# Second attention: mean squares as products of high and low parts for seven heads, each head's rows normalised in two halves

## The chip, the core and the metric

The kernel runs on one core of a Trainium2 chip. The metric is the time of one execution on the device in microseconds (us). A core has a matrix engine (PE), a vector engine (DVE), a scalar engine (ACT), a general engine (POOL) and SP, which here only issues transfers (DMA). Each engine works through its own list of instructions in order; an instruction whose input or whose buffer is not ready holds up everything behind it on that engine.

## The reference, cut to what matters

Two layers: one with latent attention, one with differential attention, each followed by a gated feed-forward layer; 1024 rows, width 1024, everything in 32 bits. The part touched is in the differential attention:

```python
a = p[:, 0] - lam * p[:, 1]                     # two softmax maps per head
o = jnp.einsum('bhqk,bkhe->bqhe', a, v)         # 8 heads, 128 values each
o = _rmsnorm(o, g_sub) * (1.0 - lambda_init)    # per row and head
# _rmsnorm: o * rsqrt(mean(o*o, axis=-1) + 1e-6) * g
return o.reshape(b, s, 1024) @ w_o
```

## The kernel before

**Products.** The matrix engine is used with two formats. A product of full 32-bit operands ("f32") and one of operands rounded to a shorter format ("fp32r") go by the same instruction; the kernel gets its accuracy from the second kind by splitting an operand into a high part (a cast, made by ACT) and a low part (the difference, made by DVE or POOL) and adding three products.

**Second attention.** It takes up 1127 to 1552 us of the span. For each of 8 heads there are 8 blocks of 128 query rows. `score_b(h, i)` makes the scores of block i for the two maps: matmuls into banks `s` (L220), a DVE instruction that adds the bias, finds the extreme and writes a score tile `l` (L223), an exponential on ACT (L228), a reciprocal of the sums (DVE L1425), a scaling of map 1 (POOL L1426) and the difference of the maps (DVE L1427), which leaves the weights of the block in the tile of map 0. `turn_b` transposes them on PE (L148) into `pt`; ACT and DVE split these into `pth` (L251) and `ptl` (L252). `mix_b` makes the value product of two blocks, a "row pair" (L263, `o_b`), and DVE copies it to `bo` (L1436). `attention()` emits the scores two blocks ahead of the transposes, and hands other work to numbered slots, one behind each block: projections of the next head (`bp`, L143 to L145) and the values of the next pair of heads (`bv`, same lines). Slot 8h+i lies behind block i of head h. What runs when is set by a scheduler that orders each engine's instructions by its own planned times; the order is fixed when the kernel is built.

**Norm.** `norm_b(h)` at slot 8h+9 squares the 128x1024 outputs of a head (ACT L1451, two instructions of 512 columns) into a tile `sq`; `norm_b2(h)` at slot 8h+10 sums over the partitions with a matmul against `ones`, a 128x128 matrix of 1/128, in f32 (L1457, `ms`, in banks `s`), takes logarithm and exponential on ACT (L1460, L1462) and multiplies on POOL (L1463), which is the last reader of `sq`. SP then stores the rows of heads 0 to 5. The last head is normalised in smaller parts at the end.

**Buffers.** The score tiles of both maps and the tiles `sq` come from one pool of five buffers, `lp`, tag `l`, 128x1024 each:

```python
lp = st.enter_context(tc.tile_pool(name="b1l", bufs=5, reuse_waits="tile"))
l = lp.tile([P, 1024], F32, tag="l", name=f"l_{name}")      # softmax_block
t = lp.tile([P, S], F32, tag="l", name=f"sq{h}_{g0}")       # norm_b
```

A score tile of map 1 is free after L1427, one of map 0 after its last transpose, a tile `sq` after the POOL multiplication. An instruction that writes a tile waits for the last reader of the buffer's tile before it.

Of the kernel before, what the change touches and what calls it, by code (L numbers as in the profile page):

```python
# [9 lines left out]
F32 = mybir.dt.float32  # L10
F32R = mybir.dt.float32r
AF = mybir.ActivationFunctionType
ALU = mybir.AluOpType
# [3 lines left out]
P = 128  # L17
S = 1024
# [3 lines left out]
H = 8  # L22
# [20 lines left out]
def trunk(  # L43
# [33 lines left out]
    V, A, G, T = nc.vector, nc.scalar, nc.gpsimd, nc.tensor  # L77

    cp = ctx.enter_context(tc.tile_pool(name="cp", bufs=1))
    sp = ctx.enter_context(tc.tile_pool(name="sp", bufs=8))  # L80

    ident = cp.tile([P, P], F32, tag="ident", name="ident")
    ones = cp.tile([P, P], F32, tag="ones", name="ones")
    cst = cp.tile([P, 48], F32, tag="cst", name="cst")
    edge = ctx.enter_context(tc.tile_pool(name="edge", bufs=1, side="right"))
    edge.tile([P, 504], F32, tag="edge", name="edge")
# [20 lines left out]
    def f32(t):  # L107
        return t.bitcast(F32)
# [1059 lines left out]


    gs, nlam = cst[:, 16:17], cst[:, 24:25]  # L1170
    V.memset(ones, 1.0 / P)

    def constants():
        nc.gpsimd.dma_start(gs, g_sub)
        V.tensor_scalar(gs, gs, 1.0 - LAMBDA_INIT, None, ALU.mult)
        t = wp.tile([P, 5, 64], F32, tag="wr", name="lv", bufs=2)
        for i, src in enumerate((lam_q1, lam_k1, lam_q2, lam_k2)):
            nc.gpsimd.dma_start(t[:, i], src.partition_broadcast(P))
        dots = t[:, 4, :2]
        for i in range(2):  # L1180
            V.tensor_tensor(t[:, 2 * i], t[:, 2 * i], t[:, 2 * i + 1], ALU.mult)
            V.tensor_reduce(dots[:, i:i + 1], t[:, 2 * i], mybir.AxisListType.X, ALU.add)
        A.activation(dots, dots, AF.Exp)
        V.tensor_tensor(nlam, dots[:, 1:2], dots[:, 0:1], ALU.subtract)
        V.tensor_scalar(nlam, nlam, -LAMBDA_INIT, None, ALU.add)


    with ast as st:
        pool = st.enter_context(tc.tile_pool(name="a1", bufs=2, reuse_waits="tile"))
        vp = st.enter_context(tc.tile_pool(name="a1v", bufs=12, side="right", reuse_waits="tile"))  # L1190
        lp = st.enter_context(tc.tile_pool(name="a1l", bufs=4, side="right", reuse_waits="tile"))
# [3 lines left out]
        vt, qr, qn, kn, wts, lt, pts = {}, {}, {}, {}, {}, {}, {}  # L1195
# [90 lines left out]
        def at(slot, fn, *args):  # L1286
            fill.setdefault(slot, []).append(lambda: fn(*args))
# [57 lines left out]
    with ExitStack() as st:  # L1345
# [2 lines left out]
        ptp = st.enter_context(tc.tile_pool(name="b1p", bufs=4, reuse_waits="tile"))  # L1348
        bb = pool.tile([P, S], F32, tag="bb", name="bb", bufs=1)
        nc.sync.dma_start(bb, c_bias_b)  # L1350
        vt, lt, pts, sqs, q_slot = {}, {}, {}, {}, {}
        qt = [big_tile(f"bq{j}") for j in range(2)]
        kt = [big_tile(f"bk{j}") for j in range(2)]
        ob = big_tile("bo", F32)
# [90 lines left out]
        def norm_b(h, g0=0, g1=4):  # L1445

            t = lp.tile([P, S], F32, tag="l", name=f"sq{h}_{g0}")
            sqs[h, g0] = [(t[:, (g - g0) * 256:min(g + 2, g1) * 256 - g0 * 256],
                           o_rows(h, g, min(2, g1 - g))) for g in range(g0, g1, 2)]
            for sq, o in sqs[h, g0]:  # L1450
                A.activation(sq, o, AF.Square)  # L1451

        def norm_b2(h, g0=0, g1=4):
            parts = []
            for i, (sq, o) in enumerate(sqs.pop((h, g0))):
                m = ps_s(f"ms{h}_{g0}_{i}")[:, :sq.shape[1]]
                T.matmul(m, ones, sq, start=True, stop=True)  # L1457
                parts.append((sq, o, m))
            for r, _, m in parts:
                A.activation(r, m, AF.Ln, bias=eps_rms, scale=1.0)  # L1460
            for r, o, _ in parts:
                A.activation(r, r, AF.Exp, scale=-0.5)  # L1462
                G.tensor_tensor(o, o, r, ALU.mult)  # L1463
            if h < H - 2:
                for g in range(g0, g1):
                    nc.sync.dma_start(o_dr[1][g][h], o_rows(h, g))
# [34 lines left out]
                for slot, tb in ((1, 0), (3, 1), (6, 2), (7, 3), (8, 4), (9, 5), (10, 6), (13, 7)):  # L1501
                    at(b + slot, values_b, h // 2, tb)
        for h in range(H - 1):
            at(8 * h + 9, norm_b, h)
            at(8 * h + 10, norm_b2, h)
        at(8 * H - 6, norm_b, H - 1, 3, 4)
        at(8 * H - 5, norm_b2, H - 1, 3, 4)
        at(8 * H - 4, norm_b, H - 1, 2, 3)
# [113 lines left out]
```

## Time and profile before

| what | value |
|---|---|
| time, median of 3 runs | 2267.78 us (2267.59 to 2267.83) |
| the profiled execution: its time | 2268.24 us |
| the profiled execution: its span in the trace | 2266.5 us, so 1.74 us lie around it |
| mean granted clock of TensorE | 0.998 of full speed |
| second attention in the span | 1127 to 1552 us |
| projection of its output, then the last feed-forward layer | from about 1505 us to the end |

The rows further down are from the profiled execution. An instruction's time there is from its start to its end, and matmuls overlap: the start of one to the start of the next is shorter than the duration printed for it. A full f32 matmul appears as two records.

### The profile page before, as it was taken

Reading aid. Unit: us, or ns where it says so; the run is one execution under the profiler, and the core shown is the slowest. Engines: PE = TensorE matmul, PEld = TensorE weight load, DVE = VectorE, ACT = ScalarE, POOL = GpSimd, SP = SyncE. Lnnn points to the kernel's source line nnn. Section 1 sums busy time; section 2 is a strip of 40 time slices with the busy share of each in tenths; the row PEclk is TensorE's granted clock in tenths of the full one; section 3 lists DMA queues with packets and bytes.
Section 4 is the critical chain, followed back from the end, with each engine's and each line's share of the span. In section 5 each row is a group of like instructions: output and inputs, shape, how many; then the busy total and the mean of one; then the engine's idle time right before and its main releaser. Section 6 shows DMA issues by size and latency. Waiting matters only on the chain.

```text
span 2266.5 us, 31066 instructions
## 1 busy us (share of the span) xinstructions
PE 2240.2 (99%) x11410; PEld 1912.8 (84%) x11410; DVE 1542.9 (68%) x2894; ACT 1014.3 (45%) x2097; POOL 773.9 (34%) x626
## 2 busy tenths in 40 slices
PE   8999999999999999999999999999999999999998
PEld 8999998888888888888888898878788888888886
DVE  5676765696766667767576667576686656668778
ACT  4365564352333334444465656564442333334444
POOL 3232341114444440455432424221114444430551
PEclk9999999999999999999999999999999999999999
DMA  5010125434435338454320212063334223238443
GB/s 203 11 37 31 42 70 186 143 127 151 174 130 204 114 129 327 183 192 158 98 52 22 68 34 64 21 223 126 125 138 163 90 103 107 100 112 324 165 180 150
DMA packets 105545, 287.76 MB, mean 127 GB/s; under 512 B 7968, under 2 KB 30112, under 8 KB 94896
## 3 DMA queue, kind: packets, MB, share of 16 engines
q1 hardware_dynamic: 101552, 277.44, 34.5%
q0 software_dynamic: 3840, 8.33, 1.4%
q8 instruction: 90, 1.47, 0.3%
q14 instruction: 63, 0.52, 0.1%
HBM read 204.47 MB, written 77.07 MB: 124 GB/s over the span
## 4 chain that ended last, share of the span: by engine, by line
PE 94%; DVE 2%; DMA 1%; issue 1%; ACT 1%; POOL 0%; SPq 0%; DVEq 0%; POOLq 0%; ACTq 0%
PE gb L548 15%; PE gc L548 10%; PE ga L548 10%; PE dw L872 7%; PE dx L872 5%; PE s_a L220 4%; PE zp_a L418 3%; PE s_b L220 3%; PE dv L872 3%; PE dy L872 3%; PE bp L145 3%; PE bp L143 3%; PE bp L144 3%; PE o_a L263 2%; PE o_b L263 2%; PE hq L1121 1%
## 5 line engine op out<-in xcount | busy, mean ns | idle before, releaser
L504 ACT CAST op_g<-gr 128x512 fp32r<-128x512 f32 x240 | 146.8, 621 | 376.9 <-PE gb L548 190.6
L505 POOL TENSOR_TENSOR op_g<-gr,op_g 128x512 fp32r<-128x512 f32 x104 | 145.5, 1404 | 255.3 <-ACT op_g L504 149.5
L505 DVE TENSOR_TENSOR op_h<-rh,op_h 128x512 fp32r<-128x512 f32 x152 | 140.7, 951 | 51.5 <-ACT op_h L504 51.5
L548 PE MATMUL ga<-xh_m,op_g 128*128 128x512 f32 x512 | 168.2, 389 | 0.0
L872 PE MATMUL dw<-op_w_t,op_h 128*128 128x512 f32 x660 | 151.1, 390 | 0.0
L504 ACT CAST op_h<-rh 128x512 fp32r<-128x512 f32 x152 | 91.9, 619 | 127.2 <-PE dx L872 35.0
L872 PEld LDWEIGHTS dw<-op_w_t,op_h 128*128 128x128 f32 x660 | 123.7, 188 | 25.6
L228 ACT ACTIVATE l_b<-l_b,mx_b 128x256 f32<-128x256 f32 (+7 forms) x128 | 99.4, 777 | 73.1 <-DVE mx_b L223 71.4
L505 POOL TENSOR_TENSOR op_w_b<-rw_b,op_w_b 128x512 fp32r<-128x512 f32 x44 | 64.4, 1488 | 172.9 <-ACT op_w_b L504 165.7
L505 DVE TENSOR_TENSOR op_g<-gr,op_g 128x512 fp32r<-128x512 f32 x136 | 111.7, 825 | 16.8 <-ACT op_g L504 16.4
L872 PE MATMUL dx<-op_w_b,op_h 128*128 128x512 f32 x528 | 121.5, 390 | 1.0 <-DVE op_w_b L505 1.0
L1426 POOL TENSOR_SCALAR l_b<-l_b,rb,cst 128x128 f32<-128x128 f32 (+3 forms) x64 | 52.5, 821 | 199.3 <-DVE rb L1425 187.9
L872 PEld LDWEIGHTS dx<-op_w_b,op_h 128*128 128x128 f32 x528 | 98.8, 188 | 23.0 <-DVE op_w_b L505 2.6
L548 PE MATMUL gb<-t3h_f,op_g 128*128 128x512 f32 x352 | 115.4, 389 | 1.4 <-DVE tmp L637 1.4
L548 PE MATMUL gb<-t2h_f,op_g 128*128 128x512 f32 x352 | 115.4, 390 | 0.4 <-DVE op_g L505 0.4
L548 PE MATMUL gc<-t1h_f,op_g 128*128 128x512 f32 x352 | 115.6, 389 | 0.0
L548 PE MATMUL gb<-t4h_f,op_g 128*128 128x512 f32 x352 | 115.5, 389 | 0.0
L548 PE MATMUL gc<-b22h_f,op_g 128*128 128x512 f32 x352 | 115.3, 389 | 0.0
L548 PEld LDWEIGHTS ga<-xh_m,op_g 128*128 128x128 f32 x512 | 96.1, 188 | 19.9
L505 POOL TENSOR_TENSOR op_g<-s,op_g 128x512 fp32r<-128x512 f32 x40 | 55.3, 1381 | 167.9 <-ACT op_g L504 159.8
L143 PE MATMUL bp<-xT_f,h_wb 128*128 128x512 f32 x256 | 101.7, 397 | 0.0
L144 PE MATMUL bp<-xT_f,h_wb 128*128 128x512 f32 x256 | 101.6, 397 | 0.0
(388 smaller groups left out, 6688.6 us busy)
## 6 DMA issues: line engine op xcount, KB each, us to landing
gr<-in_w_gu SPq DMA_DIRECT2D x44, 1024.0 KB, 6.9
rh<-h_dr SPq DMA_DIRECT2D x28, 1024.0 KB, 4.9
h_dr<-sh SPq DMA_DIRECT2D x22, 1024.0 KB, 4.9
h_dr<-hp SPq DMA_DIRECT2D x22, 768.0 KB, 4.2
tt<-in_w_dn SPq DMA_DIRECT2D x22, 512.0 KB, 7.6
rh<-h_dr SPq DMA_DIRECT2D x12, 768.0 KB, 4.4
wo_dr<-op_pwo SPq DMA_DIRECT2D x16, 512.0 KB, 3.5
z<-xs_dr SPq DMA_DIRECT2D x16, 512.0 KB, 11.5
```

Of the source, the lines that this page charges most:

```text
L143: T.matmul(ps_out, lh, rh, start=(i == 0), stop=False)
L144: T.matmul(ps_out, lh, rl, start=False, stop=False)
L145: T.matmul(ps_out, ll, rh, start=False, stop=(i == n - 1))
L220: T.matmul(s[:, :w], lh, rh[:, ks], start=(j == 0), stop=(j == len(q_pass) - 1))
L228: ends["exp"] = A.activation(l[:, :n], l[:, :n], AF.Exp, bias=mx, scale=-1.0, accum_out=sm).ins
L263: T.matmul(po[:, c], a, b[:, j % 2, c], start=st, stop=sp_, skip_group_check=True)
L418: T.matmul(m, a[:, h, :], self.wo[h][w][:, c], start=(start and h == heads[0] and a is oh and w == 0), stop=(stop and h == heads[-1] and a ...
L504: turns["cast"] = A.copy(hi, src).ins
L505: return eng.tensor_tensor(lo, src, f32(hi), ALU.subtract).ins
L548: T.matmul(o, w[:, a, k * P:(k + 1) * P], x[b][:, k, :], start=(first and k == 0 and (a, b) == (0, 0)), stop=(k == 3 and a == 1), skip_gro ...
L872: T.matmul(o, h[:, a, c], w[:, b_], start=(first and (a, b_) == (0, 0)), stop=(last and a == 1), skip_group_check=True,).ins for a, b_ in ...
L1426: G.tensor_scalar(l1[:, :n], l1[:, :n], r[:, 1:2], nlam, ALU.mult, ALU.mult)
```

## The change

Three things. `ones` becomes an fp32r tile, written by a DVE instruction from `ident` in `constants()` instead of a memset. For heads 0 to 6, each 512 columns of squares are split into a cast (ACT, L1455 of the new kernel) and a difference (DVE, L1456) in a second tile `sqhl` from the same pool `lp`; two fp32r matmuls (L1464) take the place of the f32 one. And each of these heads is normalised in two halves: row pairs 0 and 1 at slots 8h+5 and 8h+6, row pairs 2 and 3 at 8h+9 and 8h+10. A half holds 512 columns, but each of its two tiles takes a whole buffer of `lp`. The last head keeps its parts and the f32 product.

```diff
-    ones = cp.tile([P, P], F32, tag="ones", name="ones")
+    ones = cp.tile([P, P], F32R, tag="ones", name="ones")
...
-    V.memset(ones, 1.0 / P)
...
     def constants():
+        V.tensor_scalar(ones, ident, 0.0, 1.0 / P, ALU.mult, ALU.add)
...
             for sq, o in sqs[h, g0]:
                 A.activation(sq, o, AF.Square)
+                if h < H - 1:
+                    hl = lp.tile([P, S], F32R, tag="l", name=f"sqhl{h}_{g0}")
+                    hi, lo = sq_hl[h, g0] = hl[:, :512], hl[:, 512:]
+                    A.copy(hi, sq)
+                    V.tensor_tensor(lo, sq, f32(hi), ALU.subtract)
...
                 m = ps_s(f"ms{h}_{g0}_{i}")[:, :sq.shape[1]]
-                T.matmul(m, ones, sq, start=True, stop=True)
+                if h < H - 1:
+                    for k, part in enumerate(sq_hl.pop((h, g0))):
+                        T.matmul(m, ones, part, start=(k == 0), stop=(k == 1))
+                else:
+                    T.matmul(m, f32(ones), sq, start=True, stop=True)
...
         for h in range(H - 1):
-            at(8 * h + 9, norm_b, h)
-            at(8 * h + 10, norm_b2, h)
+            for i in range(2):
+                at(8 * h + (5, 9)[i], norm_b, h, 2 * i, 2 * i + 2)
+                at(8 * h + (6, 10)[i], norm_b2, h, 2 * i, 2 * i + 2)
```

The scheduler orders the whole stage anew. Two places are shown here: PE and DVE where head 1 ends, and ACT where head 6 ends. In the names, `s_b_2_0_0` is the scores of block 2, map 0, bank 0; `l_b_7_0` the tile of block 7, map 0; `pt_b_7_0` the first four transposes of block 7; the number at the end is a running number.

PE of the kernel before, where head 1 ends and head 2 begins, from the last value projections to the transposes of block 7 of head 1:

```order
L143 MATMUL bv_3_11751<-h_wbv_1_11218,xT_f_10050 128x256
L144 MATMUL bv_3_11751<-l_wbv_1_11219,xT_f_10050 128x256
L145 MATMUL bv_3_11751<-h_wbv_1_11218,xT_f_10051 128x256
L220 MATMUL s_b_2_0_0_11809<-bk_10191,bq_10189 128x384
L220 MATMUL s_b_2_0_0_11809<-bk_10191,ql_10194 128x384
L148 MATMUL pt_b_7_0_11733<-ident,l_b_7_0_11516 128x128 x4
```

PE of the changed kernel at the same place, from the scores of block 0 of head 2 to the same transposes:

```order
L220 MATMUL s_b_0_1_0_11636<-bk_10191,bq_10189 128x128
L220 MATMUL s_b_0_1_0_11636<-bk_10191,ql_10194 128x128
L1464 MATMUL ms_0_0_11728<-sqhl_0_11603,ones 128x512 x2
L220 MATMUL s_b_1_0_0_11739<-bk_10191,bq_10189 128x256
L220 MATMUL s_b_1_0_0_11739<-bk_10191,ql_10194 128x256
L220 MATMUL s_b_1_1_0_11746<-bk_10191,bq_10189 128x256
L220 MATMUL s_b_1_1_0_11746<-bk_10191,ql_10194 128x256
L220 MATMUL s_b_2_0_0_11831<-bk_10191,bq_10189 128x384
L220 MATMUL s_b_2_0_0_11831<-bk_10191,ql_10194 128x384
L148 MATMUL pt_b_7_0_11755<-ident,l_b_7_0_11525 128x128 x4
```

Before, 24 value projections (`bv_3`) stand between the scores of blocks 1 and 2 of head 2; in the changed kernel they stand earlier, and the matmuls of the first half's norm stand there instead.

DVE of the changed kernel at the same place, from the norm's difference to the difference of the maps of block 7:

```order
L1456 TENSOR_TENSOR sqhl_0_11603<-sq_0_11601,sqhl_0_11603 128x512
L252 TENSOR_TENSOR ptl_b_6_0_11651<-pt_b_6_0_11645,pth_b_6_0_11650 128x2x128
L1425 RECIPROCAL rb_7_11524<-smb_7_11523 128x2
L1436 COPY bo<-o_b_2_11606 128x256
L223 ISA l_b_0_0_11628,mx_b_0_0_0_11632<-s_b_0_0_0_11629,bb 128x128
L223 ISA mx_b_0_0_0_11632 128x1
L252 TENSOR_TENSOR ptl_b_6_1_11655<-pt_b_6_0_11645,pth_b_6_1_11654 128x2x128
L252 TENSOR_TENSOR ptl_b_6_2_11663<-pt_b_6_1_11658,pth_b_6_2_11662 128x2x128
L223 ISA l_b_0_1_11635,mx_b_0_1_0_11639<-s_b_0_1_0_11636,bb 128x128
L223 ISA mx_b_0_1_0_11639 128x1
L1427 SCALAR_TENSOR_TENSOR l_b_7_0_11525<-l_b_7_0_11525,rb_7_11524,l_b_7_1_11537 128x1024
```

The score tile `l_b_0_1` written by the last L223 lies in the buffer that held `sqhl_0_11603`; the difference of the maps of block 7 stands right behind it. Before, the buffer of that tile was one of block 6 of head 1, and L1456 was not there.

ACT of the kernel before, at the end of head 6, between the two exponentials of its block 7:

```order
L228 ACTIVATE l_b_7_0_14798,smb_7_14796<-l_b_7_0_14798,mx_b_7_0_1_14807 128x1024
L251 CAST pth_b_6_0_14922<-pt_b_6_0_14917 128x2x128
L1378 CAST bvh_7_14864<-bv_7_14839 128x256
L406 ACTIVATE oh_a_7_14957<-of_a_7_14955,cst 128x768
L228 ACTIVATE l_b_7_1_14810,smb_7_14796<-l_b_7_1_14810,mx_b_7_1_1_14819 128x1024
```

ACT of the changed kernel at the same place:

```order
L228 ACTIVATE l_b_7_0_14852,smb_7_14850<-l_b_7_0_14852,mx_b_7_0_1_14861 128x1024
L251 CAST pth_b_6_0_14981<-pt_b_6_0_14976 128x2x128
L1451 ACTIVATE sq_0_14922<-bo 128x512
L1378 CAST bvh_7_14918<-bv_7_14893 128x256
L406 ACTIVATE oh_a_7_15022<-of_a_7_15020,cst 128x768
L1455 CAST sqhl_0_14924<-sq_0_14922 128x512
L228 ACTIVATE l_b_7_1_14864,smb_7_14850<-l_b_7_1_14864,mx_b_7_1_1_14873 128x1024
```

The square and the cast of the first half of head 6 now stand ahead of the second exponential of block 7.

## Rows read from the trace of the kernel before

**Rows 1.** The profile's page: busy time, granted TensorE clock in 40 slices, chain that ended last.
```profile
PE 2240.2 (99%) x11410; PEld 1912.8 (84%) x11410; DVE 1542.9 (68%) x2894; ACT 1014.3 (45%) x2097; POOL 773.9 (34%) x626
...
PEclk9999999999999999999999999999999999999999
...
PE 94%; DVE 2%; DMA 1%; issue 1%; ACT 1%; POOL 0%; SPq 0%; DVEq 0%; POOLq 0%; ACTq 0%
```

**Rows 2.** Windows: us, busy PE, PEld, DVE, ACT, POOL, clock, DMA share, GB/s.
```profile
1480.00:1500.00 20.00, 18.62 (x112) 15.79 (x111) 17.62 (x43) 12.46 (x26) 3.41 (x4) 1.00 0.57 183
...
1127.00:1552.00 425.00, 422.31 (x2552) 372.68 (x2551) 291.92 (x814) 252.18 (x585) 137.97 (x131) 1.00 0.23 73
```

**Rows 3.** Waits of PE, 1120 to 1560 us: total, times, longest.
```profile
PE s_b L220 <- DVE mx_b L223: 0.8, 2, 0.6
PE pt_b L148 <- DVE l_b L1427: 0.8, 2, 0.6
```

**Rows 4.** Timeline of PE at two norms: start, duration, line, operation, count.
```profile
1191.07 1.07 PE L1457 MATMUL ms<-sq,ones 128*128 128x512 f32 x2
1191.58 0.80 PE L144 MATMUL bp<-xT_f,h_wb 128*128 128x512 f32 x1
1192.21 0.39 PE L145 MATMUL bp<-xT_f,l_wb 128*128 128x512 f32 x1
1192.44 0.40 PE L143 MATMUL bp<-xT_f,h_wb 128*128 128x512 f32 x1
...
1243.51 1.88 PE L1457 MATMUL ms<-sq,ones 128*128 128x512 f32 x4
1245.23 0.71 PE L148 MATMUL pt_b<-ident,l_b 128*128 128x128 f32 x5
```

**Rows 5.** ACT's groups, by shape, 1127 to 1552 us: count, busy, mean ns, idle before.
```profile
L1460 ACT ACTIVATE sq<-ms,cst 128x512 f32<-128x512 f32 x14 | 9.6, 686 | 2.1 <-PE ms L1457 2.0
L1451 ACT ACTIVATE sq<-bo 128x512 f32<-128x512 f32 x15 | 9.3, 629 | 3.1 <-DVE bo L1436 3.1
L1462 ACT ACTIVATE sq<-sq 128x512 f32<-128x512 f32 x14 | 8.7, 636 | 0.2
```

**Rows 6.** Groups of the whole span, by shape: ACT's cast, and DVE's difference.
```profile
L504 ACT CAST op_g<-gr 128x512 fp32r<-128x512 f32 x240 | 146.8, 621 | 376.9 <-PE gb L548 190.6
...
L505 DVE TENSOR_TENSOR op_h<-rh,op_h 128x512 fp32r<-128x512 f32 x152 | 140.7, 951 | 51.5 <-ACT op_h L504 51.5
...
L505 DVE TENSOR_TENSOR op_w_b<-tt,op_w_b 128x512 fp32r<-128x512 f32 x22 | 14.8, 680 | 0.0
```

**Rows 7.** POOL's multiplication, group by shape, 1127 to 1552 us.
```profile
L1463 POOL TENSOR_TENSOR bo<-bo,sq 128x512 f32<-128x512 f32 x14 | 18.8, 1350 | 6.7 <-ACT sq L1462 6.4
```

**Rows 8.** Timelines of SP, PE and DVE, up to block 7 of head 1.
```profile
1185.77 0.33 SPq L132 DMA_DIRECT2D r_wb<-in_w_b_qk  x1
...
1213.03 0.63 PE L220 MATMUL s_b<-bk,bq 128*128 128x512 f32 x2
...
1221.45 0.60 PE L148 MATMUL pt_b<-ident,l_b 128*128 128x128 f32 x4
...
1214.49 0.74 DVE L223 CUSTOM_DVE_ANT_0 l_b<-s_b,bb,mx_b 128x512 f32<-128x512 f32 x1
...
1216.81 0.29 DVE L223 CUSTOM_DVE_ANT_0 l_b<-s_b,bb 128x128 f32<-128x128 f32 x1
...
1218.57 1.27 DVE L1427 SCALAR_TENSOR_TENSOR l_b<-l_b,rb,l_b 128x1024 f32<-128x1024 f32 x1
```

**Rows 9.** Timelines of PE and ACT, block 7 of head 6, and the chain there.
```profile
1498.20 1.06 PE L148 MATMUL pt_b<-ident,l_b 128*128 128x128 f32 x8 [0.56 <-DVE l_b L1427]
...
1505.50 0.73 PE L418 MATMUL zp_a<-wo,oh_a 128*128 128x512 f32 x2 [0.77 <-DMA wo<-wo_dr]
...
1493.44 1.15 ACT L228 ACTIVATE l_b<-l_b,mx_b 128x1024 f32<-128x1024 f32 x1
...
1493.31 12.14 DMA wo<-wo_dr
```

More of the change, by code (lines that the diff above doesn't have):

```diff
@@ L1350, in trunk @@
         nc.sync.dma_start(bb, c_bias_b)
-        vt, lt, pts, sqs, q_slot = {}, {}, {}, {}, {}
+        vt, lt, pts, sqs, sq_hl, q_slot = {}, {}, {}, {}, {}, {}
         qt = [big_tile(f"bq{j}") for j in range(2)]
```

## The prediction, written before the changed kernel was run

> **What bounds the kernel now.** I read the page first. PE is busy for 99% of the span at the full clock in every slice, and the chain that ended last is PE to 94% [rows 1]. So a microsecond that PE no longer needs is a microsecond of the kernel, unless PE waits in its place; and nothing can be won on another engine. Then the windows: in the second attention PE is busy for 422.3 of 425.0 us, DVE for 291.9, ACT for 252.2, POOL for 138.0 [rows 2]. On average the other engines have room. The table of waits says where PE is idle there: 0.8 us on score tiles (L223) and 0.8 on the weights of a block (L1427) [rows 3], and with one load (0.77 [rows 9]) some 2.4 in all. The stretch from 1480 to 1500 us is the exception: PE 18.62 of 20, DVE 17.62 [rows 2]. There DVE is nearly the bound. The reader should keep these two cases apart: a stage in which PE is full and has only a few microseconds between "ready" and "needed", and a last stretch where it already waits.
>
> **What PE saves.** One f32 sum over 512 columns: from its start at 1191.07 to the start of the second matmul behind it, at 1192.21, are 1.14 us; the fp32r matmul of 512 columns between them accounts for 0.23 (1192.21 to 1192.44). That leaves 0.91. Two such sums in a row take from 1243.51 to 1245.23, or 0.86 each [rows 4]. I take 0.87; heads 0 to 6 have 14 of them, 12.2 us. The change puts 28 fp32r matmuls of the same size there, 28 x 0.23 = 6.4 us. PE saves **5.8 us**, 0.26% of the time. Bounds: 5.6 (0.86 each) to 6.3 (0.91 each).
>
> **What ACT, DVE, POOL and SP get.** ACT: 14 casts of 512 columns at 0.62 [rows 6], 8.7 us more. DVE: 14 differences of two operands in SBUF, between 0.68 and 0.95 each [rows 6], 9.5 to 13.3 us. Against the room of 173 and 133 us this is nothing on average. Squares (0.63), logarithms (0.69), exponentials (0.64) [rows 5] and POOL's multiplications (1.35) [rows 7] keep their number and size, but half of them move four blocks ahead. So do the stores of row pairs 0 and 1 of heads 0 to 5: 12 issues on SP, which wait there for POOL. For head 0 they are moved past one load of weights, issued at 1185.77 [rows 8]; their matmuls now stand 43.5 us into the stage, at about 1171, and POOL is done some 4 us later, so the load isn't held up, and I put this at nothing. The new way to fill `ones` runs on DVE in the first microseconds, long before the first use, while PE waits for its first inputs: nothing.
>
> The spread of the difference has a cause in the rows: the same form takes 0.68 where POOL does little and 0.95 in a stage where POOL does the same work beside DVE [rows 6]. The Trainium skill says in "SBUF — State Buffer", section "Who interferes with whom", that a DVE instruction with two SBUF inputs excludes a GpSimd instruction that reads SBUF; the two rows agree. By the low price the two places below would cost 0.3 us less each than by the high one; I take the middle, since POOL is busy for a third of the stage.
>
> **What the buffers cost.** This is the term that decides. Before, a head's norm held one of the five `l` buffers once. Now each half holds two: `sqhl` until its matmuls, and `sq` until POOL has multiplied. Two of five are gone, and the scores of the next blocks, which need them, come later or close behind a release. The order shows what follows at the end of head 1: the filler (24 value projections) between the last scores and the transposes of block 7 is spent earlier, and the distance on PE shrinks. Before, it was 1213.03 to 1221.45, 8.4 us, for a chain that ended when L1427 was done, at 1218.57 + 1.27 = 1219.84, so it took 6.8 and left 1.6 [rows 8]. The PE rows that now stand between take, from start to start, 0.23 for 512 columns [rows 4], 0.12 for 256 and 0.11 for a transpose, and add up to 5.0 us. The chain does not shrink. It gets longer: L1427 of block 7 stands on DVE behind L223 of block 0 of head 2, whose tile is the buffer of `sqhl`; so it can't start before the norm's matmuls, which PE reaches 1.3 us before those transposes. Behind the matmuls come L223 at 0.29 and L1427 at 1.27 [rows 8], and about 0.1 for each hand-over: 1.8 us at the least against a distance of 0.8 (four matmuls at 0.12 and two at 0.18 after the norm's). That is a wait of at least 1.0; with the cast, the square and the difference ahead of these instructions on ACT and DVE I get 2.0 from a timeline that I drew by hand. Then L223 of block 1, map 1, waits for POOL to give up `sq`: logarithm 0.69, exponential 0.64, multiplication 1.35 and the hand-overs, some 3.5 us after the matmuls. Behind it on DVE is `ptl` of block 7, which the value product of pair 3 needs: another 0.9 us of PE. I put head 1 at **2.9 us**, bounds 0.7 (only the queue of L223 and L1427 counts, with shorter hand-overs) and 3.5 (every duration at its high end).
>
> In the other six first halves the release of `sq` comes some 4 to 4.5 us after the matmuls, and the scores that use the buffer stand 4.7 to 7.5 us after them: no wait, by a small margin. The second halves are like the norm before. I count 0.4 for these, and 0.3 for block 4 of the last head, where the distance falls from 8.4 to 6.3 us.
>
> **Head 6** falls into the stretch that DVE bounds. The square (0.63) and the cast (0.62) go ahead of the second exponential of block 7, which before started at 1493.44 right behind another ACT instruction; the difference adds 0.68 to 0.95 on DVE [rows 5, 6, 9]. Everything there is late by 1.3 to 2 us. But PE also waits 0.77 us at 1505.50 for the load of `wo`, which took 12.14 us [rows 3, 9]: a delay of that size ahead of it is free, and so are the two new matmuls, which run while PE would wait. I take **0.6 us**, bounds 0 and 1.4.
>
> **Sum.** 5.8 saved, less 2.9 + 0.6 + 0.3 + 0.4 = 4.2, is 1.6 us. The profiled execution took 2268.24 (span 2266.5 and 1.74 around it), so 2266.6; it was 0.46 above the median of the runs, and against these I forecast **2266.2 us**. A measurement of this kernel can tell about 0.2%, 4.5 us, from no change: faster means below 2263.2, slower above 2272.3.
>
> **Rivals.**
> 1. The waits stay hidden, and the saving comes out whole: 2267.8 - 5.8 = 2262.0. For it: 24 fillers of 0.12 us are 2.9 us of cover, PE waited only 2.4 us in 425 before, and every wait that I add rests on an order and on prices, none on a row. It decides if all waits together stay below 1.2 us. Against it: the hand-over from the norm's matmuls over L223 to L1427 can't be made shorter than its parts. 27 in 100.
> 2. The buffers bind in every first half, not only in head 1. The margin elsewhere is 4.7 us after the matmuls at the tightest, in heads 3 and 5. If POOL's release comes later than that, because the multiplication queues behind a weight difference on POOL or the logarithm behind an exponential of 1.15 on ACT [rows 9], L223 waits and everything behind it on DVE too. With head 1, 3 and 5 at 2.9 each and 1.3 for the rest, 10.0 - 5.8 = 4.2 slower: 2272.0; with all seven, 20.3 - 5.8 = 14.5 slower: 2282. It decides from 10.3 us of waits. Against it: before, PE waited for score tiles only twice. 13 in 100. The Trainium skill, in "Perfetto Trace Analysis", section "Optimization Strategy", reads a repeated gap on the engine that should be saturated as a sign that there is no memory left for the next tile; the waits of this trace, two of each kind, show no such pattern before, and a gap at each first half would be it.
> 3. The change doesn't save what it says: two fp32r matmuls against `ones` cost more than 0.23 each, for instance 0.43 (half the f32 price). Then PE saves nothing and the waits remain: 2272. Every fp32r matmul of this size in the trace stands at 0.23, so 3 in 100, counted with rival 2's nearer case as "same" or "slower" by halves.
>
> **How the numbers follow.** My forecast, with its own bounds (4.2 of costs between 1.7 and 6.0: 2263.7 to 2268.0), has 57 in 100; rival 1 27; rival 2 13; rival 3 3. The range has to take in rival 1 whole and the near case of rival 2; it leaves out the case of seven heads: 2261.5 to 2272.0. Faster by over 0.2%: 0.27. Slower: rival 2's 13 less the part that stays below 2272.3, and half of rival 3, with some of my own upper bound: 0.13. The same: 0.60.
>
> **What would show it.** The norm's matmuls: 28 of fp32r at 0.23 between starts, and no f32 except in the last head. PE waits for `l_b` L1427 of about 2 us once, some 95 us into the stage (near 1220 us), with the value product of pair 3 waiting for `ptl` behind it. Between 1490 and 1506 us the waits for L223 and L1427 grow, and the wait for `wo` goes. If the waits of PE in the stage add up to the same 2.4 us as before, rival 1 holds; if there is a wait for L223 in each head, rival 2. I would be wrong altogether if PE's order after the stage, which also changes a little, moved more than the 0.5 us I allow for it either way.

## The result, and the profile after

The changed kernel took **2271.65 us** (median of 13 runs, 2270.16 to 2274.59) against 2267.23 for the kernel before, timed beside it (13 runs, 2266.29 to 2267.83): a ratio of 1.0021 [1.0014, 1.0028]. It is slower by 4.4 us. I had forecast 2266.2, faster by 1.6; the time lies inside my range, close to its upper end. The profiled execution took 2273.96 us with a span of 2272.2.

The page, and the windows that answer to [rows 1, 2]:

```profile
PE 2241.5 (99%) x11410; PEld 1915.9 (84%) x11410; DVE 1563.1 (69%) x2908; ACT 1020.7 (45%) x2111; POOL 771.3 (34%) x626
...
1127.00:1552.00 425.00, 415.47 (x2507) 369.04 (x2505) 305.11 (x813) 254.28 (x590) 133.66 (x130) 0.99 0.22 70
```

PE now does something for 415.5 of 425.0 us, where it did for 422.3 [rows 2]. Most of the missing 7 us stands in the waits of PE from 1120 to 1570 us (total, times, longest), 9.0 us in this list, to be held against the 2.4 us of [rows 3, 9]:

```profile
PE s_b L220 <- DVE mx_b L223: 4.4, 5, 1.4
PE o_b L263 <- ACT pth_b L251: 1.3, 1, 1.3
PE pt_b L148 <- DVE l_b L1427: 1.3, 2, 0.8
PE zp_a L418 <- DVE ptl_b L252: 0.7, 1, 0.7
PE ms L1464 <- DVE mx_b L223: 0.7, 1, 0.7
PE bv L143 <- DVE bk L1410: 0.6, 2, 0.3
```

Waits alone don't give the time, since PE can also run slower. So I cut both spans at two instructions of PE that both kernels have, the first score matmul of the stage and the last matmul of the output projection (`zp_a`):

| piece of PE's time, us | before | after | difference |
|---|---|---|---|
| start to first `s_b` | 1127.49 | 1126.32 | -1.2 |
| first `s_b` to last `zp_a` ("the stage" from here on) | 494.13 | 504.24 | +10.1 |
| last `zp_a` to the end of the last matmul | 635.16 | 631.93 | -3.2 |

The sum is +5.7, the difference of the spans. The first piece has the same instructions in both kernels; over all profiles of this study it lies between 1124.7 and 1127.5. In the last piece two waits of the kernel before are gone:

```profile
PE gb L548 <- DVE tmp L637: 1.4, 1, 1.4
PE xTp_a L148 <- DVE z_a L184: 1.3, 1, 1.3
```

For the stage I laid PE's instructions end to end by their prices from start to start (0.23 for 512 columns, 0.12 for 256, 0.86 for an f32 norm) and call **lag** what the start of a matmul is behind that sum. The prices add up to 486.4 before and 480.8 after: the 5.6 us are saved. The lag at the end is 7.7 before and 23.4 after. It grew by 1.4 at block 5 of head 1, 2.4 at the end of head 1, 1.1 in head 2, 3.5 in head 3, 1.05 in head 4, 3.5 in head 5, nothing more than before at the end of head 6, and 2.7 (before 0.3) at the end of the last head.

The norm's matmuls and its new instructions came out as priced: start, duration, then the groups (count, busy, mean ns):

```profile
1441.06 0.63 PE L1464 MATMUL ms<-sqhl,ones 128*128 128x512 f32 x2
1441.52 0.40 PE L220 MATMUL s_b<-bk,bq 128*128 128x256 f32 x2
...
L1456 DVE TENSOR_TENSOR sqhl<-sq,sqhl 128x512 fp32r<-128x512 f32 x14 | 10.0, 716 | 0.0
...
L1455 ACT CAST sqhl<-sq 128x512 fp32r<-128x512 f32 x14 | 8.7, 619 | 0.6 <-DVE l_b L1427 0.4
```

Two norm matmuls take 0.46 from start to start. What I had not priced is L1427, whose number and shapes did not change:

```profile
L1427 DVE SCALAR_TENSOR_TENSOR l_b<-l_b,rb,l_b 128x1024 f32<-128x1024 f32 x8 | 14.5, 1813 | 2.1 <-POOL l_b L1426 2.1
L1427 DVE SCALAR_TENSOR_TENSOR l_b<-l_b,rb,l_b 128x768 f32<-128x768 f32 x8 | 14.3, 1787 | 0.6 <-POOL l_b L1426 0.6
```

Before, these groups had a mean of 1278 and 1302 ns. Seven L1427 are lengthened now, by 12.5 us together (before two, by 2.9); the longest take 3.40, 3.41, 3.15 and 3.15 us. The timeline of head 3, block 7, shows how. POOL, DVE and PE of the changed kernel:

```profile
1324.21 1.20 POOL L1426 TENSOR_SCALAR l_b<-l_b,rb,cst 128x1024 f32<-128x1024 f32 x1 [6.62 <-DVE rb L1425]
1325.38 2.39 POOL L137 TENSOR_TENSOR l_wb<-r_wb,h_wb 128x1024 fp32r<-128x1024 f32 x1
...
1325.45 3.41 DVE L1427 SCALAR_TENSOR_TENSOR l_b<-l_b,rb,l_b 128x1024 f32<-128x1024 f32 x1 [0.77 <-POOL l_b L1426]
...
1330.28 0.28 DVE L223 CUSTOM_DVE_ANT_0 l_b<-s_b,bb 128x128 f32<-128x128 f32 x1
...
1330.62 0.39 PE L220 MATMUL s_b<-bk,bq 128*128 128x256 f32 x1 [1.21 <-DVE mx_b L223]
```

and the same place of the kernel before:

```profile
1322.65 1.20 POOL L1426 TENSOR_SCALAR l_b<-l_b,rb,cst 128x1024 f32<-128x1024 f32 x1 [6.72 <-DVE rb L1425]
1324.73 2.88 POOL L137 TENSOR_TENSOR l_wb<-r_wb,h_wb 128x1024 fp32r<-128x1024 f32 x1 [0.88 <-ACT pth_b L251]
...
1324.06 1.28 DVE L1427 SCALAR_TENSOR_TENSOR l_b<-l_b,rb,l_b 128x1024 f32<-128x1024 f32 x1
```

L137 is the low part of a weight of the next head (1024 columns, made by POOL). In both kernels it is the next POOL instruction behind L1426. Before, L137 stood idle for 0.88 us behind L1426 (the bracket in its row), so L1427 began 0.67 us ahead of it and kept its 1.28 us, and L137 took 2.88. After, L137 is ready when L1426 ends and began 0.07 us ahead of L1427, which waits for the same L1426; it kept its 2.39, and L1427 ended 1.09 us after it (1328.86 and 1327.77), as if it had done its work only then. In these rows whichever starts first holds up the other, and DVE is the one for which PE waits: L223, behind L1427 on DVE, is late, and with it a bank of scores. The Trainium skill says in "SBUF — State Buffer", section "Who interferes with whom", that a DVE instruction with two inputs in SBUF and a GpSimd instruction that reads SBUF exclude each other for a whole instruction, by the order of issue; these rows agree.

Behind that wait something else costs as much. Windows of 10 us around the waits of heads 3, 5 and 6, and one of 1 us (duration; busy PE, PEld, DVE, ACT, POOL; granted clock, DMA share, GB/s):

```profile
1330.00:1340.00 10.00, 9.07 (x56) 8.65 (x57) 7.07 (x26) 6.79 (x22) 2.29 (x3) 0.83 0.13 50
1440.00:1450.00 10.00, 8.50 (x54) 8.01 (x53) 7.00 (x20) 5.17 (x15) 2.56 (x4) 0.83 0.09 29
1500.00:1510.00 10.00, 7.43 (x34) 5.86 (x33) 8.33 (x24) 7.90 (x18) 2.67 (x3) 0.83 1.04 369
1333.00:1334.00 1.00, 1.00 (x7) 1.00 (x6) 0.52 (x3) 0.64 (x3) 1.00 (x1) 0.50 0.00 0
```

Before, the first two read 1.00 with PE busy for 10.00 of 10. A mean of 0.83 over 10 us is 3.4 us at 0.50, which is 1.2 instead of 2.4 GHz; where PE is full, each such stretch costs it 1.7 us. Ahead of each, PE had waited: 1.21 us in head 3, 1.19 in head 5, 1.39 and 0.68 in head 6. The value projections in the slow stretch of head 3 stand 0.21 to 0.22 us apart instead of 0.12. So in this execution a wait of 1.2 us goes with some 3 us of loss in heads 3 and 5.

At the end of head 1, by contrast, the waits are there that were forecast (PE, POOL and DVE):

```profile
1216.21 0.63 PE L220 MATMUL s_b<-bk,bq 128*128 128x512 f32 x2
...
1219.93 0.68 PE L1464 MATMUL ms<-sqhl,ones 128*128 128x512 f32 x2
...
1220.44 1.20 POOL L1426 TENSOR_SCALAR l_b<-l_b,rb,cst 128x1024 f32<-128x1024 f32 x1 [5.42 <-DVE rb L1425]
...
1221.38 0.28 DVE L223 CUSTOM_DVE_ANT_0 l_b<-s_b,bb 128x128 f32<-128x128 f32 x1
...
1221.68 1.29 DVE L1427 SCALAR_TENSOR_TENSOR l_b<-l_b,rb,l_b 128x1024 f32<-128x1024 f32 x1
...
1223.11 1.06 PE L148 MATMUL pt_b<-ident,l_b 128*128 128x128 f32 x8 [0.77 <-DVE l_b L1427]
...
1224.13 0.42 DVE L223 CUSTOM_DVE_ANT_0 l_b<-s_b,bb 128x256 f32<-128x256 f32 x1 [0.56 <-POOL bo L1472]
```

The transposes of block 7 wait for L1427, and L223 of block 1 waits for POOL's multiplication, the release of `sq`. That is the only wait for `sq` that the list of DVE's waits has for the stage. What it has of L223 waiting for a buffer, 1126 to 1570 us, changed kernel (before, only the first kind, with 0.2 us):

```profile
DVE l_b L223 <- PE pt_b L148: 0.7, 2, 0.3
DVE l_b L223 <- POOL bo L1472: 0.6, 1, 0.6
```

And the last head ends with two waits. ACT, held up for 1.36 us by POOL's multiplication, casts parts of a later weight (L504) ahead of the last two `pth`:

```profile
1548.82 0.91 ACT L406 ACTIVATE oh_a<-bo,cst 128x256 fp32r<-128x256 f32 x2 [1.36 <-POOL bo L1472]
1549.64 1.12 ACT L504 CAST op_gp<-gp 128x512 fp32r<-128x512 f32 x2
...
1551.24 0.39 PE L263 MATMUL o_b<-pth_b,bvh 128*128 128x256 f32 x1 [1.29 <-ACT pth_b L251]
1552.36 0.50 PE L418 MATMUL zp_a<-who,oh_a 128*128 128x512 f32 x1 [0.74 <-DVE ptl_b L252]
```

### The profile page after: what moved, and what is told of

It reads as the page before. It is cut to its first block, busy times and chain, and to the rows that moved or that the text cites. A ratio compares the mean times of both kernels' runs of the same rounds, so it can differ in the third digit from the quotient of the medians.

```text
span 2272.2 us, 31113 instructions
## 1 busy us (share of the span) xinstructions
PE 2241.5 (99%) x11410; PEld 1915.9 (84%) x11410; DVE 1563.1 (69%) x2908; ACT 1020.7 (45%) x2111; POOL 771.3 (34%) x626
## 5 line engine op out<-in xcount | busy, mean ns | idle before, releaser
L504 ACT CAST op_g<-gr 128x512 fp32r<-128x512 f32 x240 | 146.9, 621 | 377.0 <-PE gb L548 185.9
L504 ACT CAST op_h<-rh 128x512 fp32r<-128x512 f32 x152 | 91.9, 620 | 128.5 <-PE dx L872 35.1
L1426 POOL TENSOR_SCALAR l_b<-l_b,rb,cst 128x128 f32<-128x128 f32 (+3 forms) x64 | 52.9, 826 | 206.3 <-DVE rb L1425 189.1
L145 PE MATMUL bp<-xT_f,l_wb 128*128 128x512 f32 x256 | 101.0, 395 | 0.0
L143 PE MATMUL bp<-xT_f,h_wb 128*128 128x512 f32 x256 | 100.6, 393 | 0.2
```

The costliest lines, as they stand in the source:

```text
L143: T.matmul(ps_out, lh, rh, start=(i == 0), stop=False)
L145: T.matmul(ps_out, ll, rh, start=False, stop=(i == n - 1))
L504: turns["cast"] = A.copy(hi, src).ins
L1426: G.tensor_scalar(l1[:, :n], l1[:, :n], r[:, 1:2], nlam, ALU.mult, ALU.mult)
```

## The experiments

My theory after the result: DVE and POOL hold each other up at L1427, the norm's earlier halves having shifted who starts first, and PE's clock falls behind the waits. The main rival: the tiles `sq` and `sqhl` take two of five buffers, and score tiles come late for that (rival 2 of the prediction). Eleven kernels ran. The first two columns of times are those of the ledger above, from one profile each; "clock at 0.50" says at which us that profile shows 3.4 us of it in the stage. The median and the ratio, with the runs of the kernel before on the same chip, are from all runs. A profile is one execution: that of the changed kernel took 2.3 us more than its median, that of psum_sq 3.0 less.

| kernel | stage | behind it | clock at 0.50 | median, us | ratio |
|---|---|---|---|---|---|
| before | 494.1 | 635.2 | none | | |
| after | 504.2 | 631.9 | 1332, 1445, 1507 | 2271.65 | 1.0021 [1.0014, 1.0028] |
| apart35 | 500.3 | 631.9 | 1500, 1548 | 2269.26 | 1.0008 [0.9999, 1.0017] |
| pieces | 493.9 | 635.2 | 1496 | 2267.36 | 0.9999 [0.9990, 1.0008] |
| halves_f32 (4 runs) | 505.3 | 635.4 | 1505, 1553 | 2278.78 | 1.0046 [1.0031, 1.0062] |
| psum_sq | 495.4 | 631.8 | none | 2267.87 | 1.0000 [0.9991, 1.0009] |
| fill3 | 500.2 | 631.7 | none | 2270.86 | 1.0018 [1.0009, 1.0027] |
| pieces_h6 | 493.4 | 634.8 | none | 2265.34 | 0.9993 [0.9984, 1.0002] |
| whole3 | 492.9 | 635.6 | none | 2265.90 | 0.9997 [0.9987, 1.0006] |
| before_pieces | 500.0 | 634.9 | 1497, 1545 | 2271.52 | 1.0019 [1.0010, 1.0029] |
| ones_only | 494.4 | 635.6 | 1498 | 2267.71 | 1.0001 [0.9992, 1.0010] |
| weights_dve | 495.6 | 633.9 | 1497, 1544 | 2266.60 | 0.9999 [0.9989, 1.0008] |
| whole3_pieces | 493.6 | 631.9 | none | 2263.11 | 0.9982 [0.9973, 0.9992] |

**apart35**: the weight differences of heads 5 and 7 are tied behind a later POOL instruction; the rest of the order hardly moves.

```diff
...
+                after = {(5, 0): (4, 0), (7, 0): (6, 0)}
+                if (h, which) in after:
+                    behind(low, ends["scaled", *after[h, which]])
...
```

> The changed kernel, but on POOL the weight difference l_wb of heads 5 and 7 is ordered behind the scaling L1426 of block 0 of heads 4 and 6; the rest of the order stays almost as it is. Theory PORT: in the changed kernel's trace the difference of the maps of block 7 of heads 3 and 5 took 3.4 us instead of 1.28, because POOL's weight difference (2.39 us) began 0.07 us before it and held it up; PE then waited 1.5 us at each place, and its clock fell to half for some 3.4 us, 1.7 us more. Then those two instructions are at 1.28 again, both waits and both drops of the clock go, and the time falls by 3.0 (waits) to 6.4 us (waits and clock): 2265.3 to 2268.7. Theory BUFFERS: the waits are for the tiles that the norm holds; then nothing changes there, 2271 to 2272.

The same place in head 3 of this kernel (L1430 and L1431 are L1426 and L1427), and the windows of heads 3 and 5:

```profile
1325.69 1.28 DVE L1431 SCALAR_TENSOR_TENSOR l_b<-l_b,rb,l_b 128x1024 f32<-128x1024 f32 x1 [0.77 <-POOL l_b L1430]
1330.85 2.48 DVE L1431 SCALAR_TENSOR_TENSOR l_b<-l_b,rb,l_b 128x128 f32<-128x128 f32 x1
...
1330.78 2.40 POOL L137 TENSOR_TENSOR l_wb<-r_wb,h_wb 128x1024 fp32r<-128x1024 f32 x1
...
1330.00:1340.00 10.00, 9.82 (x75) 9.03 (x74) 9.00 (x27) 6.04 (x21) 5.32 (x5) 1.00 0.24 80
1440.00:1450.00 10.00, 9.83 (x75) 9.04 (x74) 9.01 (x25) 6.06 (x20) 5.33 (x5) 1.00 0.08 28
```

L1431 of block 7 is back at 1.28, that of block 0 is held up in its place (2.48, by itself 0.35) where PE doesn't wait for it. In all, the lengthening is no less than in the changed kernel, 13.0 us: what counts is whether PE waits behind it. The lag of heads 3 and 5 fell from 3.5 to 0.6 and 0.7, the clock stays at 1.00 there, and the stage is 3.9 us shorter in the profile, 2.4 in the medians; the other 1.8 of the 5.7 are lost again between 1507 and 1552 us, in the output projection, some 1.1 of it behind a fall of the clock at 1548 us that the profile of the changed kernel has not. 2269.26 is above the 2265.3 to 2268.7 that I had expected, and below what the buffers would give. The buffers are as in the changed kernel. This is the clearest run for the theory, as to heads 3 and 5: one instruction moved, at two places.

**pieces**: L137 in four instructions of 256 columns, so that it blocks for less.

```diff
-        j = (eng or G).tensor_tensor(lo[:, :cols], raw[:, :cols], f32(hi[:, :cols]), ALU.subtract)
+        n = 4 if name[:2] == "wb" else 1
+        for p in range(n):
+            c = slice(p * cols // n, (p + 1) * cols // n)
+            j = (eng or G).tensor_tensor(lo[:, c], raw[:, c], f32(hi[:, c]), ALU.subtract)
```

> The changed kernel, with each weight difference of the second attention (POOL, 1024 columns) made in 4 pieces of 256 columns, some 0.65 us each. Theory PORT: an instruction of DVE that meets one is held up for one piece at most, so the seven differences of the maps that were lengthened by 12.5 us in all lose most of that: waits of PE fall by some 4 to 6 us, drops of the clock go, 2264 to 2268. Theory BUFFERS: no change, 2271 to 2272.

L1427 is lengthened by 3.0 us in all instead of 12.5, and the 4.4 us are gone. But the scheduler sees four instructions and orders the stage anew, so this is not the contention alone (see before_pieces).

**halves_f32**: halves as in the change, but the f32 sum and no tile `sqhl`: one buffer for each half.

```diff
...
-                    hl = lp.tile([P, S], F32R, tag="l", name=f"sqhl{h}_{g0}")
...
-                    for k, part in enumerate(sq_hl.pop((h, g0))):
-                        T.matmul(m, ones, part, start=(k == 0), stop=(k == 1))
-                else:
-                    T.matmul(m, f32(ones), sq, start=True, stop=True)
+                T.matmul(m, f32(ones), sq, start=True, stop=True)
```

> The changed kernel without the split: half a head at a time, squares summed by an f32 matmul as before, one buffer held per half instead of two. PE saves nothing. Theory BUFFERS: the waits fall to those of the kernel before, 2266.5 to 2268. Theory PORT: POOL's order is what moved (one multiplication per half instead of two per head), so POOL's weight differences meet L1427 as in the changed kernel: waits and drops of the clock as there and 5.8 us of PE on top, 2272 to 2278.

If the second tile were the cause of the loss, this kernel would have come back to 2266.5 to 2268. It is the slowest of all, 0.8 us above what the theory gave; eight L1427 are lengthened, by 13.3 us, and heads 3 and 5 have a lag of 1.5 each, at full clock. The wait at the end of head 1 is gone, though (lag 0.2), so for that place this run does not clear the second tile. L1427 of 1024 columns:

```profile
L1427 DVE SCALAR_TENSOR_TENSOR l_b<-l_b,rb,l_b 128x1024 f32<-128x1024 f32 x8 | 14.5, 1809 | 2.3 <-POOL l_b L1426 2.3
```

**psum_sq**: squares and their factor in a PSUM bank instead of `sq`, and the last multiplication on DVE instead of POOL.

```diff
-            t = lp.tile([P, S], F32, tag="l", name=f"sq{h}_{g0}")
+            t = ps_s(f"sq{h}_{g0}") if h < H - 1 else lp.tile([P, S], F32, tag="l", name=f"sq{h}_{g0}")
...
-                G.tensor_tensor(o, o, r, ALU.mult)
+                (V if h < H - 1 else G).tensor_tensor(o, o, r, ALU.mult)
```

> The changed kernel with the squares of the first seven heads in a PSUM bank instead of a tile of the score pool, logarithm and exponential in the bank of the sum, and the last multiplication on DVE (about 0.7 us) instead of POOL: per half one buffer, and only until the sum is made. Theory BUFFERS: the wait of some 2 us at the end of head 1 goes, and those at heads 3 and 5, 2263 to 2267. Theory PORT: what remains depends on where POOL's weight differences fall; the waits at heads 3 and 5 stay if they begin with L1427 of block 7, 2267 to 2272.

No L1427 is lengthened, and the stage takes 495.4, in the fastest execution of this kernel (2264.83). The end of head 1 still has 4.2 us of lag. The median of 2267.87 lies in the theory's range by 0.9 us and as much above that of the buffers. This run changes buffers, POOL and order at once, so it doesn't tell the theories apart by itself.

**fill3**: the norm's two matmuls made three times in the first halves of heads 3 and 5 (only the last pass counts; 0.92 us more for PE in each), to fill the wait there.

```diff
-                    for k, part in enumerate(sq_hl.pop((h, g0))):
-                        T.matmul(m, ones, part, start=(k == 0), stop=(k == 1))
+                    parts_hl = sq_hl.pop((h, g0))
+                    for n in range(3 if h in (3, 5) and g0 == 0 else 1):
+                        for k, part in enumerate(parts_hl):
+                            T.matmul(m, ones, part, start=(k == 0), stop=(k == 1))
```

> The changed kernel with the pair of matmuls of the first half's norm made three times over in heads 3 and 5 (the same sum, written again): 0.92 us more work on PE at each of the two places where PE waited 1.2 us and its clock then fell. The late instruction on DVE, and so the end of the wait, stays where it is. Theory CLOCK: the drop of the clock to half follows from PE's idle time; with most of it filled there is no drop at these places, and the time falls by up to 1.7 us for each in executions that had both: 2268.5 to 2270.5. If the drop doesn't come from the idle time, it stays and the time is that of the changed kernel or more, 2271 to 2273.

Windows of heads 3 and 5 in this kernel:

```profile
1330.00:1340.00 10.00, 9.41 (x69) 8.71 (x68) 8.02 (x28) 6.85 (x21) 2.28 (x3) 1.00 0.22 76
1440.00:1450.00 10.00, 9.41 (x69) 8.68 (x68) 8.31 (x25) 5.89 (x18) 2.28 (x3) 1.00 0.09 29
```

L1427 is lengthened by the same 12.5 us, but PE waits 0.28 where it waited 1.21, the clock stays at 1.00, and the lag of each place is about 1.1 instead of 3.5, or 2.0 with the 0.92 of added work. The difference of 1.5 fits the 1.7 that a fall of the clock costs a full PE. That the filling kept the clock up is not shown by one profile, since a fall can come in one execution and not in another (ones_only). In the medians little is left of it, 0.8 us, less than the intervals tell. So in the other runs either the clock of the changed kernel falls less often than its profile shows, or this kernel loses elsewhere; the granted clock of its runs doesn't decide it.

**whole3**: the split product alone, a head at a time as before; a norm holds three of the five buffers.

```diff
...
-            for i in range(2):
-                at(8 * h + (5, 9)[i], norm_b, h, 2 * i, 2 * i + 2)
-                at(8 * h + (6, 10)[i], norm_b2, h, 2 * i, 2 * i + 2)
+            at(8 * h + 9, norm_b, h)
+            at(8 * h + 10, norm_b2, h)
```

> The split product alone: the two fp32r matmuls, but whole heads at the old slots, with one tile of squares and two of high and low parts, so three of the five buffers at a time. Theory BUFFERS: two buffers are left for the scores while a norm is on its way, PE waits for score tiles in every head, 7 times 1 to 3 us, less 5.7 saved: 2268 to 2283. Theory PORT: POOL multiplies two halves in a row as before, its weight differences keep their places, few of them meet L1427, and the saving comes out: 2261 to 2264.

With more buffers taken than in the change, the stage is the shortest of all, 492.9. Together with halves_f32 this refutes the buffers as the main cause. They are not without effect: DVE waits longer here for tiles that the transposes must free, 6.1 us against 0.7 in the changed kernel,

```profile
DVE l_b L223 <- PE pt_b L148: 6.1, 6, 2.1
```

and 2265.90 misses the 2261 to 2264 that the theory gave: of the 5.6 us that PE saves, 1.2 come out in the stage. At the end of head 1 PE waits 1.0 us for an L1427 of 1.28 us, without any race.

The four kernels make a square. Stage: by whole heads 494.1 (f32) and 492.9 (split), by halves 505.3 and 504.2, of which falls of the clock make up to 3.4 and 5.1. Medians, against the kernel before: whole heads 0 and -0.9, halves +11.6 and +4.4. **The halves lose time with either product**, 11 us of stage in the profiles, 11.6 (f32) and 5.3 (split) in the medians. What the split is worth depends on the order that comes with it: by whole heads some 1 us, by halves 1.1 in the profiled stages and 7.2 in the medians (behind the stage, the profiles differ by another 3.5). These runs don't separate how much the halves need in any order and how much is this order's: apart35 took back 4 of the 11 in its profile by moving two instructions.

**pieces_h6**: pieces, and the first half of head 6 four blocks later.

```diff
...
+                late = 0 if i else 4 if h == 6 else 0
...
```

> The kernel with POOL's weight differences in 4 pieces, and the first half of head 6 normalised beside its second (slots 8h+9 and 8h+10) instead of four blocks earlier, out of the stretch around 1500 us where ACT and DVE are full. If that half costs there what its square, cast and difference take ahead of the second exponential of block 7, the waits of 1.4 + 0.7 + 0.5 us and the drop of the clock at that place shrink by about 1.3 to 3 us: 2264 to 2266. If the stretch is bound by DVE whatever stands there, as in the kernel before, no change: 2267.

2265.34, as expected, against 2267.36 of pieces on another chip; their intervals overlap, so the 2 us are not shown. No fall of the clock in its profile.

**before_pieces**: the kernel before with L137 in pieces, and nothing else.

> The kernel before with POOL's weight differences in 4 pieces. Its trace has one difference of the maps that was lengthened, by 2.3 us, without a wait of PE. So no change by any theory, 2266 to 2268.5; what it differs from that by is what a new order of the stage alone does.

I had expected no change, and it lost 4.7 us. This run is the control that the others need: an edit that takes nothing from PE and adds nothing to it reorders the stage, and the new order costs 5.8 us there, 1.3 of them at the end of head 1. Its waits of PE name other instructions than those of the changed kernel:

```profile
PE pt_b L151 <- DVE ptl_b L255: 1.5, 2, 0.9
PE o_b L266 <- ACT pth_b L254: 1.3, 1, 1.3
PE s_b L223 <- DVE mx_b L226: 1.1, 3, 0.5
PE zp_a L421 <- DVE ptl_b L255: 0.7, 1, 0.7
```

Its clock stood at 0.50 for 6.8 us in all, which is up to 3.4 of the 5.8. The waits of `o_b` and `zp_a` are those at the end of the last head of the changed kernel (its lines stand three further down), here without any part of the change. So an order alone can make that end, without the halves or the split.

**ones_only**: the kernel before with `ones` written by DVE; every engine's order is otherwise unchanged.

```diff
-    ones = cp.tile([P, P], F32, tag="ones", name="ones")
+    ones = cp.tile([P, P], F32R, tag="ones", name="ones")
...
-    V.memset(ones, 1.0 / P)
...
+        V.tensor_scalar(ones, ident, 0.0, 1.0 / P, ALU.mult, ALU.add)
...
-                T.matmul(m, ones, sq, start=True, stop=True)
+                T.matmul(m, f32(ones), sq, start=True, stop=True)
```

> The kernel before, with only the new way to fill the matrix of 1/128 (fp32r, from DVE, read as f32 by the same matmuls). The order of all other instructions is that of the kernel before. By every theory no change: 2266.5 to 2268. If the part ahead of the second attention is 1 us shorter here too, as it was in the changed kernel, that came from this edit.

No difference, as forecast. Its profile has a fall of the clock at 1498 to 1501 us that the profile of the kernel before, with the same order and nearly the same waits of PE there, has not: the fall differs from one execution to the next. In that stretch, where PE waits for DVE in any case, it cost little: the stage is 0.3 us longer.

**weights_dve**: the changed kernel with L137 of heads 2 to 7 on DVE, so that POOL can't be ahead.

```diff
-                wts[which, h] = load_w(w_b_qk[h, which], 1024, f"wb{h}_{which}")
+                wts[which, h] = load_w(w_b_qk[h, which], 1024, f"wb{h}_{which}", eng=V if h > 1 else None)
```

> The changed kernel, with the weight differences of the projections of heads 2 to 7 on DVE instead of POOL: 12 differences of 1024 columns, about 1.3 us each, 16 us more on DVE, which has 120 us to spare in the stage. Theory PORT: nothing on POOL is left that can hold a difference of the maps up for 2 us (the multiplications of the norm can, by about 1), the lengthening falls from 12.5 to under 4 us, the waits in heads 1 to 5 and the drops of the clock at heads 3 and 5 go: 2263 to 2268, unless DVE is now late somewhere else. Theory BUFFERS: 2271 or more, since DVE only gets more to do.

```profile
L1427 DVE SCALAR_TENSOR_TENSOR l_b<-l_b,rb,l_b 128x1024 f32<-128x1024 f32 x8 | 10.2, 1276 | 0.3 <-POOL l_b L1426 0.2
```

L1427 of 1024 columns is back at 1276 ns (four of 128 columns are still lengthened, by 3.5 us), and the loss is gone although DVE, the busier engine, has more to do. The lag of heads 2 to 5 is 0.1, 0.8, 0.2 and 0.8, where it was 1.1, 3.5, 1.05 and 3.5. That points to POOL's weight differences in heads 2 and 4 as well, though the order is made anew here too. The end of head 1 still has 1.7.

**whole3_pieces**: whole3 with L137 in pieces.

> The split product alone, with whole heads at the old slots and three of five buffers held, and POOL's weight differences in 4 pieces. The split product alone took 2265.9 with 7.8 us of lengthened differences of the maps, the pieces took the changed kernel from 2271.7 to 2267.4. Theory PORT: lengthening falls to about 3 us; but little of it was waited for in the split product alone, so 2264 to 2266. As the order of the stage is made anew, the wait at the end of the last head (0.3 to 4.7 us in the runs so far) may move it by 2 us either way.

2263.11, ratio 0.9982: faster than both kernels, by 4 us against before. I had expected 2264 to 2266, with the lengthening down to 3 us; it is 8.4, against 7.7 in whole3. The stage is not shorter either (493.6 and 492.9); in the profiles the gain lies in the last feed-forward, where the two waits shown above are gone. So it is a faster kernel, but not by less lengthening of L1427.

## Why the prediction went wrong

**PE's saving** was right: 5.8 forecast, 5.6 by the starts of the norm's matmuls in the two traces. Cast 0.619 (0.62), difference 0.716 (between 0.68 and 0.95) and `ones` (nothing) were right too, and rival 3 is refuted by two norm matmuls in 0.46 us.

**The end of head 1** was right in size, 2.4 for 2.9, and by half in its path. The distance on PE shrank and the release of `sq` holds L223. But the chain did not get longer: from the last scores (1216.21) to the end of L1427 (1222.97) it took 6.8 us, as before. L1427 does stand right behind the L223 that needs the buffer of `sqhl`, but the norm's matmuls had freed that buffer at 1220.61, before DVE came to this L223 (1221.38), and L1427 could not have started before POOL's L1426 was done, at 1221.64, in any case. whole3 and before_pieces have waits at this place as well (lag 2.1 and 1.3), so the size was in part luck. The 0.4 us for the other small places did not include 1.4 at block 5 of head 1, where an L1427 of 768 columns took 2.92 instead of 1.01.

**The step that failed** is "In the other six first halves [...] no wait, by a small margin". I had looked only at the buffer `sq`, and for that the sentence holds: DVE waited for `sq` once, in head 1. But heads 3 and 5 cost 3.5 us each, because L1427 lost by 0.07 us a race with POOL's weight difference, and heads 2 and 4 some 1.1 each. With the 1.4 in head 1 that is 10.5 us where I had 0.4. I had read [rows 6] as a spread of 0.27 us in one instruction's price. The row of 0.95 is a mean of two kinds, as its shortest, median and longest duration show (ns, kernel before):

```profile
L505 DVE TENSOR_TENSOR op_h<-rh,op_h x152: 674/683/4455, 858.5 to 2243.0; 128x512 fp32r<-128x512 f32 x152
```

Most take 0.68 us, and about a quarter take longer, up to 4.5. For L1427 the price of being held up is up to 2.1 us, and it falls where DVE has no time to lose. Rival 2 had these two heads at 2.9 each and 2272.0 for the sum: the right places and nearly the right time, for a wrong reason. The Trainium skill, in "Perfetto Trace Analysis", section "Optimization Strategy", says that a repeated gap can mean missing memory for the next tile; the gap did repeat, in heads 3 and 5, but halves_f32 and whole3 show that memory was not its cause here.

**The clock** was no term at all, since it stood at 1.00 in the stage before [rows 2]. It doubled the price of the waits in heads 3 and 5 in the profiled execution. The thirteen runs point the same way: those with a granted clock of 0.998 took 2270.16 to 2271.87, those with 0.996 or 0.997 took 2273.29 to 2274.59.

**Head 6** was costed at 0.6 (0 to 1.4). Its stretch has 4.7 us of lag and had 4.6 before: the waits moved from the load of `wo` to L223 and L1427, as described, at no price.

**The ends.** I gave the last head 0.3, and its end costs 2.4 more than before. I allowed 0.5 either way for the order behind the stage; it gave back 3.2. Both come from the order that the scheduler made, and before_pieces and whole3_pieces have the one and the other without the change's halves.

In sums: 5.6 saved, 15.7 of new lag in the stage against my 4.2 (up to 5.1 of it by the three falls of the clock), 3.2 and 1.2 given back outside it, which is the +5.7 of the two profiled spans; the medians differ by 4.4. My bounds for the costs, 1.7 to 6.0, were not the sums of the bounds of the terms, which are 1.4 and 5.6; neither pair reaches the measured cost. **Open** is how often an execution has the falls of the clock. The race itself was taken away in apart35, and not forced in the kernel before. And why the scheduler's order comes out with or without the waits at the two ends, and at the end of head 1, was not traced.

## What to carry to other kernels

Where an engine that is awaited has instructions with two SBUF inputs, look on POOL for long instructions that may begin just before them: here a shift of less than a microsecond decided who waited, moving the long one took 2.4 us back, and giving it to another engine the whole loss. Read a group's median beside its mean: the mean of 0.95 us above stood for instructions of 0.68 and of up to 4.5. When a change makes a scheduler order a stage anew, time a neutral edit that also reorders it, as before_pieces here (4.7 us), before a few microseconds are put down to the change. Of two edits that come together, run each alone: here the halves lost in both products, and the split by whole heads did not.

## What the hardware showed that I had not expected

An L1427 of 128 columns, 0.35 us by itself, took 2.48 behind a POOL subtraction of 2.40 that began 0.07 us before it: nearly the whole length of the other is lost, not a share. And waits of 1.2 to 1.4 us in a PE that was otherwise full were followed by 3.4 us at 1.2 GHz in heads 3, 5 and 6, while the 1.3 and 0.7 us at the end of the last head of the same trace, and in fill3 a wait of 2.5 us for `wo`, were not.
